# The opening of a hybrid attention block, from the norm to the rotary product, as named pieces in a written order

## The chip, the core and the metric

The kernel runs on one core of a Trainium2 chip. A core has five engines that run side by side: TensorE (PE) for matmuls, with its weight loads shown as PEld; VectorE (DVE), ScalarE (ACT) and GpSimd (POOL) for everything elementwise; SyncE (SP), which here issues transfers (DMA). Each engine works through its own list in order and waits for the others by semaphores. Matmul results land in PSUM; the other data lies in SBUF. The metric is the device time of one execution in microseconds; a profile shows one such execution.

## What is computed

One decoder layer with two attention branches over 528 tokens (16 meta tokens, then 512 real ones) of width 1024, in fp32:

```python
u = rmsnorm(h, pre_norm_g)
proj = u @ w_in
(cq, ckv, k_pe_raw, z_mla, fq, fk, fv, f_logit, z_fox, gate_a, gate_b) = jnp.split(proj, split_idx, axis=-1)
q = rmsnorm(cq, mla_q_norm_g) @ w_uq          # 16 heads, 64 plain + 32 rotary
kv = rmsnorm(ckv, mla_kv_norm_g) @ w_ukv
o_mla = causal_block_attention(q_m, k_m, v_mla, MLA_SCALE)
y_mla = (o_mla * silu(z_mla)) @ w_br_mla
cum = cumsum(log_sigmoid(f_logit + fox_forget_b))
o_fox = causal_block_attention(fq, fk, fv, FOX_SCALE, cum)
y_fox = (o_fox * silu(z_fox)) @ w_br_fox
mixed = (sigmoid(gate_a) * y_mla + sigmoid(gate_b) * y_fox) @ w_out
h = h + rmsnorm(mixed, post_norm_g)
```

## The kernel before

Products are made in split precision: an operand is cast to a rounded high half on ACT (`wh`, `uTh`, L142, L379), the difference is its low half (`wl`, `uTl`, made by `split_lo`, L118), and each product is three matmuls: high by high, low by high, high by low. All matmuls are recorded in the helper at L92, all PE transposes at L95, so the profile's tile names tell them apart.

The **opening** runs up to the first attention scores (`st`). It treats the tokens in five tiles: 0 to 3 with 128 real tokens each, 4 with the 16 meta tokens.

- `front(t)` (L351) sums the squares of a tile's rows on ACT (L361, L367), takes the root, multiplies the rows by its reciprocal and by the gain vector `gb` on DVE (`hn`, L370), turns them by eight PE transposes (`pt`) and splits the result into `uTh` and `uTl`.
- `gb` is the gain vector read from DRAM once for each of the 128 partitions, by two transfers ahead of the first weights (L320).
- `back(t)` (L382) multiplies a tile with the 432 columns of the small projection (q rank, kv rank, rotary key, forget gate) into `psm`: 24 matmuls, for each of eight k the three passes. These weights come in four loads of two k each (`wsr`, L326), with halves `wsh` and `wsl`. Then come the norms of the two ranks and the rotation of the key (`sm`, `tm`), and four transposes back (`pc`), from which `cTh`, `cTl`, `kpT` (rotary key) and `fT` (forget gate) are filled.
- Steps of head pair 0's query and key (`fq`, `fk`, eight k with three matmuls each; `fk` in two halves of the tokens) are run between the last tiles.
- The forget gate's cumulative sum (`fa`, L427 to L435) is stored to `CT`, which the fourth set of score matmuls reads.
- Behind that come the values of pair 0 (`v`, with a power-of-two scale from the largest value, L606 to L614), one output gate (`pg`, with its tanh) and the rotary part of eight heads' queries (`ppe`), whose four products with the rotary table are made on DVE (`gT`, L561).

Weights of 1024 columns come by `wload` (L120) into three slots (`wraw`) that the first three tiles of x also use; `wsplit` (L138) makes the halves, the low one on POOL unless told otherwise. Loads are asked for a few units ahead.

In the opening, a scheduler orders each engine's list, by the order in which the code is written and by the priorities given (`high_priority`). From the first attention stage on, PE's list is as written, and in the first stage the other engines' lists too.

Of the kernel before, what the change touches and what calls it, by code (L numbers as in the profile page):

```python
# [54 lines left out]
def block_kernel(ctx: ExitStack, tc: tile.TileContext, x, meta_tokens, pre_norm_g, w_in, fox_forget_b,  # L55
# [236 lines left out]
    lctx = ExitStack()  # L292
    with ExitStack() as ph:
        pa = ph.enter_context(tc.tile_pool(name="pa", bufs=2))
        pa1 = ph.enter_context(tc.tile_pool(name="pa1", bufs=1))
        pal = lctx.enter_context(tc.tile_pool(name="pal", bufs=1, side="right"))
        ppt = ph.enter_context(tc.tile_pool(name="ppt", bufs=2, space=PSUM))
        pps = ph.enter_context(tc.tile_pool(name="pps", bufs=2, space=PSUM, side="right"))
        warm = pa1.tile([1, 16], F32, tag="warm", name="warm")
        nc.scalar.activation(warm[:, 0:1], eps_t[0:1, 0:1], AF.Sqrt)  # L300

        hts = {}
        halves = (slice(0, 512), slice(512, D))

        def load_h(t):

            pool, tag = (wp, "wraw") if t < 3 else (pa, "ht")
            hts[t] = pool.tile([128, D], F32, tag=tag, name=f"ht{t}")
            if t == 0:
                for sl in halves:  # L310
                    nc.sync.dma_start(hts[t][:, sl], x2[0:128, sl])
            elif t < 4:
                nc.sync.dma_start(hts[t], x2[128 * t : 128 * t + 128])
            else:
                nc.sync.dma_start(hts[t][0:META], meta_tokens)

        load_h(0)
        gb = pa1.tile([128, D], F32, tag="gb", name="gb")
        for sl in halves:
            nc.sync.dma_start(gb[:, sl], pre_norm_g[0:1, sl].broadcast_to([128, 512]))  # L320
        wsh = pa1.tile([128, KD, NSM], F32R, tag="wsh", name="wsh")
        wsl = pa1.tile([128, KD, NSM], F32R, tag="wsl", name="wsl")
        nsm0 = NSM - NH
        for c in range(4):
            r = pa.tile([128, 2, NSM], F32, tag="wsr", name=f"wsr{c}", bufs=4)
            nc.sync.dma_start(r[:, :, 0:nsm0], win[:, 2 * c : 2 * c + 2, 0:nsm0])  # L326
            nc.sync.dma_start(r[:, :, nsm0:], win[:, 2 * c : 2 * c + 2, O_F : O_F + NH])
            if c == 1:
                load_h(1)
            hi = wsh[:, 2 * c : 2 * c + 2, :]  # L330
            nc.scalar.copy(hi, r)
            split_lo((nc.gpsimd, nc.vector)[c % 2], wsl[:, 2 * c : 2 * c + 2, :], r, hi)
        for t in (4, 2, 3):
            load_h(t)
        gq = pa1.tile([128, R_Q + R_KV], F32, tag="gq", name="gq")
        nc.sync.dma_start(gq[:, 0:R_Q], mla_q_norm_g[0:1].broadcast_to([128, R_Q]))
        nc.sync.dma_start(gq[:, R_Q:], mla_kv_norm_g[0:1].broadcast_to([128, R_KV]))
        rt = pa1.tile([128, 5, 4, 16], F32, tag="rt", name="rt")
        nc.sync.dma_start(rt, rope_tok)
        fb = pa1.tile([NH, 1], F32, tag="fb", name="fb")  # L340
        nc.sync.dma_start(fb, fox_forget_b.rearrange("a h -> h a"))
        fa = pal.tile([NH, 3, L], F32, tag="fa", name="fa")
        nc.gpsimd.memset(fa[:, 2], 0.0)
        fT = pal.tile([NH, L], F32, tag="fT", name="fT")
        kpT = pal.tile([ROPE, L], F32, tag="kpT", name="kpT")

        def rstd(dst, ss, n, epsc, rows):
            nc.scalar.activation(dst, ss, AF.Sqrt, bias=eps_t[:rows, epsc : epsc + 1], scale=1.0 / n)
            nc.vector.reciprocal(dst, dst)

        def front(t):  # L351
            rows, d0 = (128, META + 128 * t) if t < 4 else (META, 0)
            ht = hts[t]
            hn = pa.tile([128, D], F32, tag="hn", name=f"hn{t}")
            st1 = pa.tile([128, 16], F32, tag="st1", name=f"st1_{t}")
            parts = [slice(0, D)]
            if t == 0:

                parts = halves
                for i, sl in enumerate(parts):  # L360
                    nc.scalar.activation(hn[:, sl], ht[:, sl], AF.Square, accum_out=st1[:, 2 + i : 3 + i])  # L361
                nc.vector.tensor_scalar(out=st1[:, 0:1], in0=st1[:, 2:3], scalar1=1.0 / D, scalar2=EPS, op0=ALU.mult,
                                        op1=ALU.add)
                nc.scalar.activation(st1[:, 1:2], st1[:, 3:4], AF.Sqrt, bias=st1[:, 0:1], scale=1.0 / D)
                nc.vector.reciprocal(st1[:, 1:2], st1[:, 1:2])
            else:
                nc.scalar.activation(hn[:rows], ht[:rows], AF.Square, accum_out=st1[:rows, 0:1])  # L367
                rstd(st1[:rows, 1:2], st1[:rows, 0:1], D, 0, rows)
            for sl in parts:
                nc.vector.scalar_tensor_tensor(out=hn[:rows, sl], in0=ht[:rows, sl], scalar=st1[:rows, 1:2],  # L370
                                               in1=gb[:rows, sl], op0=ALU.mult, op1=ALU.mult)
            for half in range(2):
                pt = ppt.tile([128, 4, 128], F32, tag="pt", name=f"pt{t}_{half}")
                for kk in range(4):
                    k = 4 * half + kk
                    tps(pt[:, kk, :rows], hn[:rows, 128 * k : 128 * k + 128], ident[:rows, :rows])
                dh = uTh[:, 4 * half : 4 * half + 4, d0 : d0 + rows]
                dl = uTl[:, 4 * half : 4 * half + 4, d0 : d0 + rows]
                nc.scalar.copy(dh, pt[:, :, :rows])  # L379
                split_lo(nc.vector, dl, pt[:, :, :rows], dh)  # L380

        def back(t):  # L382

            rows, d0, q0 = (128, META + 128 * t, 0) if t < 4 else (META, 0, R_Q)
            psm = pps.tile([128, NSM], F32, tag="psm", name=f"psm{t}")
            passes(psm[:, q0:], lambda k: uTh[:, k, d0 : d0 + 128], lambda k: uTl[:, k, d0 : d0 + 128],
                   lambda k: wsh[:, k, :], lambda k: wsl[:, k, :], KD, slice(q0, NSM))
            sm = pa.tile([128, NSM], F32, tag="sm", name=f"sm{t}")
            st2 = pa.tile([128, 16], F32, tag="st2", name=f"st2_{t}")
            for a, b, i in ((0, R_Q, 0), (R_Q, R_Q + R_KV, 1)):  # L390
                if a < q0:
                    continue
                nc.scalar.activation(sm[:rows, a:b], psm[:rows, a:b], AF.Square, accum_out=st2[:rows, i : i + 1])
                rstd(st2[:rows, 2 + i : 3 + i], st2[:rows, i : i + 1], b - a, 0, rows)
                nc.vector.scalar_tensor_tensor(out=sm[:rows, a:b], in0=psm[:rows, a:b], scalar=st2[:rows, 2 + i : 3 + i],
                                               in1=gq[:rows, a:b], op0=ALU.mult, op1=ALU.mult)
            k0 = R_Q + R_KV
            tm = pa.tile([128, 2, 2, 16], F32, tag="tm", name=f"tm{t}")
            for i in range(2):
                for cs in range(2):  # L400
                    nc.vector.tensor_tensor(out=tm[:rows, i, cs], in0=psm[:rows, k0 + 16 * i : k0 + 16 * i + 16],
                                            in1=rt[:rows, t, 2 * i + cs], op=ALU.mult)
# [16 lines left out]
        for f, t in ((front, 0), (front, 1), (back, 0), (front, 4), (front, 2), (back, 1), (front, 3), (back, 2)):  # L419
            f(t)  # L420
        run(qk[:3])
        back(3)
        run(qk[3:7])
        back(4)


# [816 lines left out]
```

## Time and profile before

| | |
|---|---|
| runs shown | 623.45, 625.56, 625.99 us (median 625.56) |
| the profiled execution | 623.18 us, of it 621.3 us span |
| granted TensorE clock | 0.997 |
| first transpose on PE | 7.78 us |
| first scores (`st`) on PE | 72.45 us |
| bytes moved | 85.15 MB, 137 GB/s over the span |

In the profile's rows a time is in microseconds from the span's start. A timeline row gives start, duration, engine, line, operation, what it writes and reads, and in brackets how long the engine stood idle before it and what ended that. A row of stretches gives the length, the busy time of PE, PEld, DVE, ACT and POOL (each with its number of instructions), the granted clock, the share of time that the DMA engines were busy, and GB/s.

### The profile page before, as it was taken

To read this page: it belongs to the slowest core of one execution; us is meant where nothing else is said; L and a number is where in the kernel's file an instruction comes from. 1 tells how busy PE (TensorE), PEld (TensorE's weight loads), DVE (VectorE), ACT (ScalarE), POOL (GpSimd) and SP (SyncE) were. 2 spreads that over 40 slices of the span, in tenths; PEclk is the share of its full clock that TensorE was granted. 3 is DMA by queue.
4 is the path that set the end of the run, shared out by engine and by line. 5 is a ranking of instruction groups with operands and counts; after the bars stand their busy time and mean duration, and the time that the engine had idled before them with its cause. 6 is when DMAs were issued, how large, how long until landed. Compare 5 with 4: busy or idle time off the path is not lost.

```text
span 621.3 us, 11569 instructions
## 1 busy us (share of the span) xinstructions
PE 600.1 (97%) x4058; PEld 492.9 (79%) x4058; DVE 381.8 (61%) x1015; ACT 384.0 (62%) x838; POOL 188.9 (30%) x237
## 2 busy tenths in 40 slices
PE   3999999999999999999999999999999999999996
PEld 2879787978988889889889888887888865565885
DVE  3746668367466566674774774676977865556133
ACT  5656677379477576774884784776767654444421
POOL 3234544634444353352444353420000000003700
PEclk9999999999999999999999999999999999999998
DMA  8442576876666577467357586567252137332202
GB/s 284 129 85 52 128 139 175 188 192 163 161 136 140 142 148 157 125 167 180 97 142 172 137 145 161 137 162 216 66 157 80 35 89 250 101 111 93 102 34 103
DMA packets 204842, 85.15 MB, mean 137 GB/s; under 512 B 122788, under 2 KB 197924, under 8 KB 204784
## 3 DMA queue, kind: packets, MB, share of 16 engines
q1 hardware_dynamic: 204784, 84.41, 53.7%
q8 instruction: 32, 0.52, 0.4%
q14 instruction: 26, 0.21, 0.1%
HBM read 54.95 MB, written 4.00 MB: 95 GB/s over the span
## 4 chain that ended last, share of the span: by engine, by line
PE 88%; ACT 3%; DMA 3%; DVE 3%; POOL 2%; issue 1%; SPq 0%; DVEq 0%; ACTq 0%; POOLq 0%
PE pg L92 14%; PE z L92 13%; PE v L92 8%; PE st L92 7%; PE po L92 7%; PE fq L92 7%; PE fk L92 7%; PE py L92 6%; PE ov L92 5%; PE yx L92 3%; PE psm L92 3%; DMA wraw<-in_w_in_dram 2%; PE yy L92 2%; PE mq L92 2%; ACT wh L142 1%; PE mk L92 1%
## 5 line engine op out<-in xcount | busy, mean ns | idle before, releaser
L118 POOL TENSOR_TENSOR wl<-wraw,wh 128x1024 fp32r<-128x1024 f32 (+1 forms) x60 | 133.0, 2219 | 299.2 <-ACT wh L142 288.3
L142 ACT CAST wh<-wraw 128x1024 fp32r<-128x1024 f32 (+1 forms) x74 | 72.9, 986 | 84.8 <-issue 35.3
L708 ACT ACTIVATE sf<-sf,nb 128x144 f32<-128x144 f32 (+3 forms) x128 | 71.9, 565 | 3.4 <-DVE nb L698 3.4
L736 ACT ACTIVATE pn<-sf,ri 128x128 f16<-128x128 f32 (+3 forms) x128 | 61.9, 551 | 15.2 <-ACT sf L708 13.8
L737 DVE SCALAR_TENSOR_TENSOR pn<-sf,ri,pn 128x128 f16<-128x128 f32 (+3 forms) x128 | 65.6, 554 | 7.4 <-ACT pn L736 7.4
L92 PE MATMUL pg<-uTh,wh 128*128 128x512 f32 x128 | 51.9, 406 | 0.0
L92 PE MATMUL z<-uTh,wh 128*128 128x512 f32 x128 | 50.9, 398 | 0.0
L92 PE MATMUL z<-uTh,wl 128*128 128x512 f32 x128 | 50.1, 392 | 0.0
L92 PE MATMUL z<-uTl,wh 128*128 128x512 f32 x128 | 50.1, 391 | 0.0
L92 PE MATMUL pg<-uTh,wl 128*128 128x512 f32 x128 | 50.0, 391 | 0.0
L92 PE MATMUL pg<-uTl,wh 128*128 128x512 f32 x128 | 49.9, 390 | 0.0
L92 PE MATMUL st<-hlk,hlq 64*128 64x272 f32 (+3 forms) x480 | 48.6, 307 | 1.1 <-DVE nb L698 0.9
L698 DVE CUSTOM_DVE_ANT_0 sf<-st,maskt 128x272 f32<-128x272 f32 (+2 forms) x128 | 48.4, 434 | 0.0
L92 PE MATMUL py<-g,yw 128*128 128x512 f16 x192 | 42.6, 379 | 0.6 <-DVE yw L1006 0.6
L92 PEld LDWEIGHTS st<-hlk,hlq 64*128 64x128 f32 x480 | 35.7, 185 | 8.1 <-DVE nb L698 2.6
L92 PE MATMUL fk<-uTl,wh 128*128 128x256 f32 (+1 forms) x128 | 36.6, 286 | 0.0
L92 PE MATMUL v<-uTh,wh 128*128 128x256 f32 (+1 forms) x128 | 36.5, 285 | 0.0
L92 PE MATMUL fk<-uTh,wh 128*128 128x256 f32 (+1 forms) x128 | 36.5, 285 | 0.0
L92 PE MATMUL fk<-uTh,wl 128*128 128x256 f32 (+1 forms) x128 | 36.5, 285 | 0.0
L92 PE MATMUL v<-uTl,wh 128*128 128x256 f32 (+1 forms) x128 | 36.4, 285 | 0.0
L92 PE MATMUL v<-uTh,wl 128*128 128x256 f32 (+1 forms) x128 | 36.4, 285 | 0.0
L92 PEld LDWEIGHTS <-yw 128*128 128x128 f16 x192 | 17.8, 97 | 22.7 <-DVE yw L1006 1.1
(291 smaller groups left out, 1503.3 us busy)
## 6 DMA issues: line engine op xcount, KB each, us to landing
wraw<-in_w_in_dram SPq DMA_DIRECT2D x56, 512.0 KB
yraw<-in_w_br_fox_dram SPq DMA_DIRECT2D x8, 512.0 KB
yraw<-in_w_br_mla_dram SPq DMA_DIRECT2D x8, 512.0 KB
wraw<-in_w_out_dram SPq DMA_DIRECT2D x8, 512.0 KB
pt<-pn SPq DMA_TRANSPOSE x128
xr<-in_x_dram SPq DMA_DIRECT2D x4, 512.0 KB
out_dram<-yo SPq DMA_DIRECT2D x8, 256.0 KB
QP<-qpe_dram SPq DMA_DIRECT2D x7, 256.0 KB
```

The costliest lines, as they stand in the source:

```text
L92: nc.tensor.matmul(*a, **k)
L118: eng.tensor_tensor(out=lo, in0=src, in1=f32(hi), op=ALU.subtract)
L142: nc.scalar.copy(wh[:, :n], raw[:, :n])
L698: nc.vector.tensor_tensor_reduce(out=sf_of(h, b)[:, c0 : c0 + w], in0=ps[h][:, o : o + w], in1=maskt[:, m0 : m0 + w], scale=-scale, scalar ...
L708: nc.scalar.activation(sf, sf, AF.Exp, bias=sums["nb"][:, h, b : b + 1], scale=-1.0, accum_out=sums["su"][:, h, b : b + 1])
L736: nc.scalar.activation(hi, sf, AF.Copy, scale=rib)
L737: nc.vector.scalar_tensor_tensor(out=lo, in0=sf, scalar=rib, in1=hi, op0=ALU.mult, op1=ALU.subtract)
```

## The change

The scheduler no longer orders the opening. Every step is a small function with a name, and three lists of names (`OPENING`, `MIDDLE`, `LAST`; 205, 48 and 4 names) are run through in order, with all five engines' lists as issued. `front` and `back` become a class `Tile` with one method for each piece. The names: `Sq` sum of squares, `sr` root, `hn` scaled rows, `pt` transposes of half a tile (a, b), `uh`/`ul` the halves of u, `wh`/`wl` with a digit the halves of the small weights' four parts, `hh`/`lh`/`hl` two matmuls of the small projection (u's half, weight's half, tile, part), `qs qn ks kn tm kc` the norms, rotation and gate columns, `pc` the transposes back, `ch cl kf` what is filled from them; `L`, `wh`, `wl` with a letter q, k, v, g, p, z the load and halves of a large weight.

```diff
+    OPENING = (
+        "Sq0a Sq0 rc0 hn0a wh0 hn0b Lq pt0a wl0 uh0a pt0b wh1 ul0a hh00 uh0b wl1 lh01 Sq1 hl00 ul0b hl01 sr1 "
+        "wh2 hn1 Lk hh01 wh3 hh02 lh02 wl3 lh03 Sq4 wl2 hh03 pt1a sr4 pt1b hn4 uh1a hl03 Sq2 hh10 hl11 ul1a "
...
+        "lh30 kf2 fq5 cl2 qs3 tm3 fq6 ks3 qn3 fq7 kc3 kn3 fk10 hq fk11 pc3 whg lq fk12 fk13 kf3 wlg fk14 fk15 "
+        "ch3 fk16 ab fk17 cl3"
+    ).split()
+    MIDDLE = (
+        "Lz Lr ex v00 kph v01 mem v02 v03 v04 v05 hk1 v06 lnf v07 v10 lk1 v11 vr0 v12 v13 whp st v14 v15 wlp "
+        "v16 v17 scan pg0 whz pg1 vr1 chc pg2 wlz vs pg3 chl Lm Lb vT pg4 kpl pg5 vz pg6 pg7"
+    ).split()
...
+        ph.enter_context(tc.manual_schedule(engines={E_.PE, E_.Activation, E_.DVE, E_.Pool, E_.SP}))
...
+        grow = pa1.tile([1, D], F32, tag="grow", name="grow")
+        nc.scalar.dma_start(grow, pre_norm_g[0:1])
...
+        dark = acc("dark")
+        for _ in range(4):
+            mm(dark, ALL1, ALL1.unsqueeze(1).broadcast_to([128, 4, 128]), start=True, stop=True)
+        gb = [acc(f"gb{i}") for i in range(2)]
+        for i, sl in enumerate(halves):
+            mm(gb[i], one, grow[:, sl], start=True, stop=True)
...
+        for name in OPENING:
+            do[name]()
```

Four things change beside the order. The gain vector is loaded as one row (`grow`) on ACT's queue and spread over the partitions by two plain fp32 matmuls with a column of ones, into two PSUM buffers that hold it until tile 3 is scaled; the spread load is gone. Four bf16 matmuls of ones with ones (`dark`), whose result nothing reads, stand first on PE. The low halves of the weights of query, key, value, gate and rotary product, and of the third part of the small weights, are made on DVE instead of POOL. The z weight of the first attention stage is loaded and split ahead of that stage instead of in it.

The list of SP, which issues the loads, began so before:

```order
L311 DMA ht_125<-in_x_dram 128x512 x2
L320 DMA gb<-in_pre_norm_g_dram 128x512 x2
L326 DMA wsr_133<-in_w_in_dram 128x2x416
L327 DMA wsr_133<-in_w_in_dram 128x2x16
L326 DMA wsr_138<-in_w_in_dram 128x2x416
L327 DMA wsr_138<-in_w_in_dram 128x2x16
L313 DMA ht_141<-in_x_dram 128x1024
```

and begins now, still on SP at the program's start:

```order
L450 DMA ht_131<-in_x_dram 128x512 x2
L461 DMA wsr_134<-in_w_in_dram 128x2x416
L462 DMA wsr_134<-in_w_in_dram 128x2x16
L461 DMA wsr_137<-in_w_in_dram 128x2x416
L462 DMA wsr_137<-in_w_in_dram 128x2x16
L452 DMA ht_140<-in_x_dram 128x1024
```

The two transfers of `gb` are gone; the weights' first part follows x directly.

PE's list began with tile 0's transposes and took each k's three passes in turn:

```order
L95 MATMUL pt_0_181<-ident,hn_172 128x128 x4
L95 MATMUL pt_1_188<-ident,hn_172 128x128 x4
L92 MATMUL psm_215<-wsh,uTh 128x432
L92 MATMUL psm_215<-wsl,uTh 128x432
L92 MATMUL psm_215<-wsh,uTl 128x432
L92 MATMUL psm_215<-wsh,uTh 128x432
```

and now, at the same place:

```order
L92 MATMUL gb_173<-grow,one 128x512
L92 MATMUL gb_174<-grow,one 128x512
L95 MATMUL pt_0_189<-ident,hn_177 128x128 x4
L95 MATMUL pt_1_196<-ident,hn_177 128x128 x4
L92 MATMUL psm_203<-wsh,uTh 128x432 x2
L92 MATMUL psm_203<-wsh,uTl 128x432 x2
L92 MATMUL psm_203<-wsl,uTh 128x432 x4
L92 MATMUL psm_203<-wsh,uTh 128x432 x4
L92 MATMUL psm_203<-wsh,uTl 128x432 x4
L92 MATMUL psm_203<-wsh,uTh 128x432 x2
L95 MATMUL pt_0_241<-ident,hn_210 128x128 x4
L95 MATMUL pt_1_247<-ident,hn_210 128x128 x4
```

The order within a tile now follows the halves: 18 of tile 0's products stand ahead of tile 1's transposes, where 13 stood before, and the low weights come when their part is split.

On ACT, which makes the high halves, the rows behind tile 0's sum of squares were:

```order
L331 CAST wsh<-wsr_133 128x864
L331 CAST wsh<-wsr_138 128x864
L379 CAST uTh<-pt_0_181 128x4x128
L379 CAST uTh<-pt_1_188 128x4x128
L367 ACTIVATE hn_195,st_1_196<-ht_141 128x1024
```

and are now:

```order
L489 CAST wsh<-wsr_134 128x864
L554 CAST uTh<-pt_0_189 128x4x128
L489 CAST wsh<-wsr_137 128x864
L554 CAST uTh<-pt_1_196 128x4x128
L529 ACTIVATE hn_210,st_1_211<-ht_140 128x1024
```

The first half of tile 0 is cast as soon as the first part of the weights is, ahead of the second part.

More of the change, by code (lines that the diff above doesn't have):

```diff
@@ L288, in k_fox @@
         return unit(f"fk{pr}", win_w(O_FK, pr), u_act, KD, ALLT, done)
[L292 to L402, printed above, removed]
-            nc.vector.tensor_tensor(out=sm[:rows, k0 : k0 + 32].rearrange("p (a b) -> p a b", a=2), in0=tm[:rows, 0],
-                                    in1=tm[:rows, 1], op=ALU.add)
-            nc.scalar.copy(sm[:rows, k0 + 32 :], psm[:rows, k0 + 32 :])
-            pc = pps.tile([128, 4, 128], F32, tag="pc", name=f"pc{t}", bufs=1)
-            i0 = q0 // 128
-            for i in range(i0, 3):
-                tps(pc[:, i, :rows], sm[:rows, 128 * i : 128 * i + 128], ident[:rows, :rows])
-            tps(pc[0 : ROPE + NH, 3, :rows], sm[:rows, k0:NSM], ident[:rows, :rows])
-            ds = slice(d0, d0 + rows)
-            nc.scalar.copy(cTh[:, i0:3, ds], pc[:, i0:3, :rows])
-            split_lo(nc.vector, cTl[:, i0:3, ds], pc[:, i0:3, :rows], cTh[:, i0:3, ds])
-            nc.scalar.copy(kpT[:, ds], pc[0:ROPE, 3, :rows])
-            nc.scalar.activation(fT[:, ds], pc[ROPE : ROPE + NH, 3, :rows], AF.Identity, bias=fb)
-        qk = q_fox(0) + k_fox(0)
[L419 to L424, printed above, removed]
-        nc.scalar.activation(fa[:, 0], fT, AF.Abs)
-        nc.scalar.activation(fa[:, 0], fa[:, 0], AF.Exp, scale=-1.0)
-        nc.scalar.activation(fa[:, 0], fa[:, 0], AF.Ln, bias=1.0)
-        nc.vector.scalar_tensor_tensor(out=fa[:, 1], in0=fT, scalar=0.0, in1=fa[:, 0], op0=ALU.min, op1=ALU.subtract)
-        nc.vector.tensor_tensor_scan(out=fa[:, 0], data0=fa[:, 1], data1=fa[:, 2], initial=0.0, op0=ALU.add,
-                                     op1=ALU.add)
-        ch = pal.tile([NH, 2, L], F32R, tag="ch", name="ch")
-        nc.scalar.activation(ch[:, 0], fa[:, 0], AF.Copy, scale=-1.0 / SC_FOX)
-        nc.vector.scalar_tensor_tensor(out=ch[:, 1], in0=fa[:, 0], scalar=-1.0 / SC_FOX, in1=f32(ch[:, 0]),
-                                       op0=ALU.mult, op1=ALU.subtract)
-        for i in range(2):
-            for h in range(2):
-                nc.sync.dma_start(f32(CT[64 * h + i : 64 * h + i + 1, :]), f32(ch[h : h + 1, i]))
-        for i in range(2):
-            nc.sync.dma_start(c_dram[i], f32(ch[:, i]))
-        run(qk[7:])
@@ L473, in __init__, with put, fn, rope_w @@
             self.steps[0][1].load = w.load
-    E_ = mybir.EngineType
+    later = {}
+    def put(names):
+        def fn(i, *fns):
+            later.update(zip(names[i], fns))
+        return fn
+    q0, k0 = q_fox(0, put([("hq", "lq")])), k_fox(0, put([("hk0", "lk0"), ("hk1", "lk1")]))
+    g0 = gate_unit()
+    wv0 = win_w(O_FV, 0)
+    wuqh = wuq.rearrange("p k (h e) -> p k h e", e=NOPE + ROPE)
+    def rope_w(g):
+        return weights(lambda: [wuqh[:, k, 8 * g : 8 * g + 8, NOPE + 16 * x : NOPE + 16 * x + 16]
+                                for x in range(2) for k in range(2)], lambda ws: ws)
@@ new lines, in block_kernel, with hi, fn, lo @@
+    wp0 = rope_w(0)
+    lows, made = {}, {}
+    def hi(name, make, eng):
+        def fn():
+            lows[name] = []
+            made[name] = make(eng, lows[name])
+        return fn
+    def lo(name):
+        def fn():
+            for f in lows[name]:
+                f()
+        return fn
+    for name, get, make, eng in (("q", q0[0][1], q0[0][1].make, nc.vector), ("k", k0[0][1], k0[0][1].make, nc.vector),
+                                 ("v", wv0, wv0, nc.vector), ("g", g0[0][1], g0[0][1].make, nc.vector),
+                                 ("p", wp0, wp0, nc.vector)):
+        later.update({"L" + name: get.load, "wh" + name: hi(name, make, eng), "wl" + name: lo(name)})
@@ new lines, in block_kernel, with ab, ex, lnf @@
+    for k in range(KD):
+        later[f"fq{k}"] = q0[k][1]
+        later[f"pg{k}"] = g0[k][1]
+        for i in range(2):
+            later[f"fk{i}{k}"] = k0[KD * i + k][1]
+    def ab():
+        nc.scalar.activation(fa[:, 0], fT, AF.Abs)
+    def ex():
+        nc.scalar.activation(fa[:, 0], fa[:, 0], AF.Exp, scale=-1.0)
+    def lnf():
+        nc.scalar.activation(fa[:, 0], fa[:, 0], AF.Ln, bias=1.0)
+    def st_():
+        nc.vector.scalar_tensor_tensor(out=fa[:, 1], in0=fT, scalar=0.0, in1=fa[:, 0], op0=ALU.min, op1=ALU.subtract)
@@ L556, in pe_unit @@
             for xi in range(2):
[L557 removed]
+                get = (lambda: half(1)) if xi else get0 and (lambda: half(0, get0())) or weights(srcs, lambda ws: half(0, ws))
                 def done(i, ps, xi=xi):
@@ L812, in block_kernel @@
         mgates = [Gate() for _ in gates[:]]
-        ahead(first + sum(fills, []) + tail + mgates[0].steps)
-        run(first)
+        za, q, zb = early
+        later.update(whz=hi("z", za.make, nc.gpsimd), wlz=lo("z"), Lz=za.load, Lm=q.load, Lb=zb.load, mem=mem, kph=kph,
+                     kpl=kpl, Lr=lambda: nc.sync.dma_start(rope0_t, rope_pe))
+        for k in range(KD):
+            for i in range(2):
+                later[f"v{i}{k}"] = v0[KD * i + k][1]
+        with tc.manual_schedule(engines={E_.PE, E_.SP, E_.Pool, E_.Activation, E_.DVE}):
+            for name in MIDDLE:
+                later[name]()
+            lctx.close()
+            gT = [gctx[b].enter_context(tc.tile_pool(name=f"gp{b}", bufs=1, side="right")).tile(
+                [128, KD, S], F32, tag=f"gT{b}", name=f"gT{b}") for b in range(2)]
+            pe, *rope0 = pe_unit(0, lambda: made["p"])
+            for x in range(2):
+                for k in range(2):
+                    later[f"pp{x}{k}"] = pe[2 * x + k][1]
+            for name in LAST:
+                later[name]()
+        pe, pe_turn, pe_rest, _ = pe_unit(1)
+        fills[1][9:9] = pe + [(0, pe_turn)] + [(0, lambda x=x: pe_rest(x)) for x in (1, 0)]
+        ahead(sum(fills, []) + tail + mgates[0].steps)
         late = []
```

323 lines of the change are left out of this document (270 added, 53 removed), and 6 rows, old and new, of the table OPENING.

## The prediction, made before the changed kernel had run

> **What bounds the kernel now.** I read the page first: its busy line and the chain that ended last.
>
> ```profile
> span 621.3 us, 11569 instructions
> PE 600.1 (97%) x4058; PEld 492.9 (79%) x4058; DVE 381.8 (61%) x1015; ACT 384.0 (62%) x838; POOL 188.9 (30%) x237
> ...
> PE 88%; ACT 3%; DMA 3%; DVE 3%; POOL 2%; issue 1%; SPq 0%; DVEq 0%; ACTq 0%; POOLq 0%
> ```
>
> The reader sees a kernel that TensorE (PE) carries throughout: 621.3 - 600.1 = 21.2 us of its span hold no matmul. Next come the busy times by stretch. The opening ends at 72.45, where the first scores (st) start.
>
> ```profile
> 0.00:20.00 20.00, 9.20 (x30) 7.59 (x31) 9.18 (x11) 9.55 (x17) 7.43 (x16) 1.00 0.88 289
> 20.00:72.45 52.45, 50.71 (x306) 44.09 (x304) 32.13 (x82) 32.77 (x84) 17.54 (x17) 1.00 0.33 81
> ```
>
> The first figure behind the length is PE's: half of the 21 us without a matmul (20 - 9.20 = 10.8) lies in the first 20 us, and only 1.74 in the 52 us behind it. So the change, which ends at the first scores, can win much only at the very start. PE's timeline there shows a second loss:
>
> ```profile
> 7.78 2.04 PE L95 MATMUL pt<-ident,hn 128*128 128x128 f32 x8 [7.78 <-DVE hn L370]
> 12.05 0.73 PE L92 MATMUL psm<-wsh,uTh 128*128 128x432 f32 x1 [2.23 <-ACT uTh L379]
> ...
> 13.98 0.73 PE L92 MATMUL psm<-wsh,uTl 128*128 128x432 f32 x1 [0.79 <-DVE uTl L118]
> 14.50 0.56 PE L92 MATMUL psm<-wsh,uTh 128*128 128x432 f32 x1
> 14.86 0.56 PE L92 MATMUL psm<-wsl,uTh 128*128 128x432 f32 x1
> ...
> 18.10 1.91 PE L95 MATMUL pt<-ident,hn 128*128 128x128 f32 x8
> ...
> 20.08 0.36 PE L92 MATMUL psm<-wsh,uTl 128*128 128x432 f32 x1
> 20.27 0.36 PE L92 MATMUL psm<-wsh,uTh 128*128 128x432 f32 x1
> ```
>
> Equal products start 0.36 us apart at 14.5 and 0.19 at 20: up to about 20 PE runs at half speed, though the granted clock reads 1.00. It speeds up after 6.1 us without a pause (13.98 to 20.08). By 20.08 fourteen products and 16 transposes had started, and the twentieth ends near 21.25 (six more by 0.195). I use that point, **tile 0's 20th product with two tiles transposed**, as the mark of comparison. Behind it come these pauses:
>
> ```profile
> 29.71 0.66 PE L95 MATMUL pt<-ident,hn 128*128 128x128 f32 x4 [0.25 <-DVE uTl L118]
> ...
> 30.84 0.66 PE L95 MATMUL pt<-ident,hn 128*128 128x128 f32 x4 [0.28 <-DVE uTl L118]
> ...
> 33.30 0.41 PE L95 MATMUL pc<-ident,sm 128*128 128x128 f32 x2 [0.24 <-DVE sm L395]
> ...
> 37.40 0.27 PE L95 MATMUL pc<-ident,sm 128*48 128x128 f32 x1 [0.80 <-DVE sm L403]
> ...
> 46.52 0.41 PE L95 MATMUL pc<-ident,sm 128*128 128x128 f32 x2 [0.15 <-DVE sm L395]
> ```
>
> Together 1.72 us: 0.53 for a transpose buffer (pt), 1.19 for a token tile's normed row (sm). From the mark to st, 72.45 - 21.25 = 51.2 us, PE therefore works 49.5.
>
> **The change, part by part.** *The gain vector (gb) comes by two matmuls instead of a spread load.* Rows of VectorE (DVE), two stretches whose last number is GB/s, rows of ScalarE (ACT), POOL and DVE:
>
> ```profile
> 5.07 0.16 DVE L365 RECIPROCAL st<-st 128x1 f32<-128x1 f32 x1 [0.79 <-ACT st L364]
> 6.88 0.75 DVE L370 SCALAR_TENSOR_TENSOR hn<-ht,st,gb 128x512 f32<-128x512 f32 x1 [1.65 <-DMA gb<-in_pre_norm_g_dram]
> ```
> ```profile
> 2.00:3.00 1.00, 0.00 (x0) 0.00 (x0) 0.00 (x0) 0.20 (x1) 0.08 (x1) 1.00 0.99 371
> 4.00:5.00 1.00, 0.00 (x0) 0.00 (x0) 0.15 (x1) 0.97 (x5) 0.00 (x0) 1.00 0.51 111
> ```
> ```profile
> 3.38 0.63 ACT L361 ACTIVATE hn<-ht 128x512 f32<-128x512 f32 x1 [1.17 <-DMA ht<-in_x_dram]
> ...
> 9.38 0.91 ACT L331 CAST wsh<-wsr 128x864 fp32r<-128x864 f32 x1 [4.35 <-DMA wsr<-in_w_in_dram]
> ...
> 11.42 1.06 ACT L379 CAST uTh<-pt 128x512 fp32r<-128x512 f32 x2
> 12.37 1.07 ACT L367 ACTIVATE hn<-ht 128x1024 f32<-128x1024 f32 x1
> ```
> ```profile
> 10.38 2.03 POOL L118 TENSOR_TENSOR wsl<-wsr,wsh 128x864 fp32r<-128x864 f32 x1 [8.30 <-ACT wsh L331]
> ```
> ```profile
> 13.24 1.27 DVE L118 TENSOR_TENSOR uTl<-pt,uTh 128x512 fp32r<-128x512 f32 x2
> ...
> 14.62 1.29 DVE L370 SCALAR_TENSOR_TENSOR hn<-ht,st,gb 128x1024 f32<-128x1024 f32 x1
> ```
>
> DVE has its scale at 5.23 and waits for gb until 6.88. Meanwhile DMA falls from 371 to 111 GB/s. Without those 0.52 MB the first weights (wsr, 0.44 MB at 370) follow x directly: x lands by 4.0, weights at about 5.2 instead of 9.38, the next every 1.2 us, each tile of x 1.4. The one-row load (grow) is smaller than half of x, which lands at 3.38; I take that as its end. No row shows a plain fp32 product: between 0.43 us (432 columns in 0.36, for 512) and 1.02 (a transpose of 128 columns in 2.04/8). I take 1.02, as it too is fp32: both are done at 5.4, ahead of the 5.98 at which PE is wanted, so they cost nothing. The four warming products (dark) lie ahead of them.
>
> [...]
>
> *The walk to the mark*, each piece at its row's price. hn 5.23 to 5.98 and 6.7; transposes (0.255 each) to 7.0 and 8.0. ACT: wh0 to 6.1, uTh 7.0 to 7.5, wh1 8.4, uTh 8.9, square of tile 1 and root 10.2, wh2 11.1, wh3 12.0, then tile 4's square to 13.3. POOL's wsl: 6.1 to 8.2. DVE: wl1 8.4 to 9.5, hn of tile 1 10.2 to 11.6, wl3 12.0 to 13.1. PE: first product at **7.5** (12.05 before), the second pair at 8.4, and from there no pause: pairs of 0.72 end at 9.1, 9.9, 10.6, 11.3, 12.0, 12.7, 13.5, 14.2. If the speed again comes after 6.1 us without a pause, it comes at 14.5; tile 1's transposes end near 15.2 and the 20th product at **15.6**. That is 21.25 - 15.6 = **5.65 us** won.
>
> [...]
>
> *The low halves of five weights, and one more of the small ones, go from POOL to DVE.*
>
> ```profile
> 81.92 1.21 DVE L118 TENSOR_TENSOR wl<-wraw,wh 128x1024 fp32r<-128x1024 f32 x1
> ```
> ```profile
> 24.27 0.67 PE L95 MATMUL pt<-ident,hn 16*128 16x16 f32 x8
> ...
> 51.65 0.29 PE L92 MATMUL fk<-uTh,wh 128*128 128x272 f32 x1
> 51.77 0.29 PE L92 MATMUL fk<-uTl,wh 128*128 128x272 f32 x1
> ```
>
> Four such, one of half the width and one of 864 columns are 6.4 us more on DVE. DVE is busy 32.13 of the 52.45 us, so they fit; what they can do is delay a piece behind them. From 12.0 on, DVE's row up to tile 3's hn is wl3, wl2, hn4, two uTl, hn2, wlq, wlk, hn3 and 0.3 of small ones: 1.0 + 1.0 + 1.4 + 1.3 + 1.4 + 1.2 + 1.2 + 1.4 + 0.3 = 10.2, with some 0.7 of waits 22.9. PE comes to that transpose at 15.6 + fourteen pairs at 0.39 + tile 4's transposes 0.67 + tile 2's 1.0 (half of 1.91) + six fk pieces of three at 0.12 = 24.9. Cover: 2 us; beyond it each us costs one.
>
> *The pauses behind the mark.* The two waits on pt (0.53) go: between a tile's halves the list puts other products. For the waits on sm I see no row of the new order, so bounds: 0, as the list has 2.8 to 3.1 us of products ahead of the pc of tiles 2 and 3, and twice today's 1.19. I take 1.19 again, the value of the rows of that kind: **0.53 us** won.
>
> *The forget-gate chain* (fa, L427 to L435, then CT), with the scale of v that now stands ahead of its end:
>
> ```profile
> 54.89 0.65 ACT L427 ACTIVATE fa<-fT 16x528 f32<-16x528 f32 x1
> ...
> 64.09 0.40 PE L92 MATMUL pg<-uTh,wh 128*128 128x512 f32 x1
> ...
> 64.93 0.70 DVE L435 SCALAR_TENSOR_TENSOR ch<-fa,ch 16x528 fp32r<-16x528 f32 x1 [0.71 <-ACT ch L434]
> ...
> 66.97 0.16 DVE L614 RECIPROCAL vsc<-vsc 128x1 f32<-128x1 f32 x1
> ...
> 72.45 0.56 PE L92 MATMUL st<-hlk,hlq 64*128 64x144 f32 x6
> ```
> ```profile
> L440 SPq DMA_DIRECT2D CT<-ch x4: 534/583/638, 64.9 to 66.9; - x4
> ```
>
> 10.7 us from start to end; st follows 6.8 later. In the list its last step stands behind the peak of v's second half, and v ends 8.4 us ahead of st (64.09 to 72.45 are gate and rotary product). Peak and scale at most 1.5 (65.63 to 67.13), this step 0.7, two of CT's issues 1.2, a landing under 3.4 (x's, from the program's start): 6.8. Cover: at least 1.6 us. Table loads, kpT copies (KPH) and the z weight's halves, now ahead of st, lie beside v and pg. Behind st all engines keep their order but for one cast and one load, so the rest moves as a whole.
>
> **Sum:** 5.65 + 0.53 = 6.2 us. The profiled execution took 623.18, so 617.0. That execution is 2.4 under the median of the runs shown, 625.56 (623.45 to 625.99); by the median it would be 619.4. I predict the middle, **618.0**.
>
> **Rivals.** (a) *The half speed lasts*: if pauses reset it and it ends only at 18, the mark comes at 17.0; 4.3 + 0.5 = 4.8 won, 618.4 (620.8 by the median). For it: the 2.23 us pause before 12.05. Against: from 8.4 on nothing pauses. (b) *In-order rows give part back*: each ACT and DVE piece now waits at the head of its row. Fourteen handovers behind the mark (six half tiles, five pc, three psm buffers) at 0.2 us (the small pauses above are 0.15 to 0.28) cost 2.8: 3.4 won, 619.8. (c) *Hidden anyway*: PE arrives early but st waits for CT; should the chain overrun its cover by 4.5 us, 1.7 are won, 621.5. Against: the cover, and a landing that is far smaller than x's. (d) *Slower*: v's weight (Lv) loads only when tile 2's hn has freed its slot, at 18.8, and its cast stands in ACT's row ahead of tiles 0 and 1's norms and tile 3's uTh. In before loads queued on slots long:
>
> ```profile
> SPq L133 <- POOL wl L118: 31.3, 6, 17.3
> ```
>
> Landing after 24.9 costs PE us for us; past 31.1 the whole gain is gone. A 17.3 us hold there means landing near 39, 14.1 late: 7.9 lost net, 631.1. Against: the slot is freed by DVE, whose row has cover, and DMA moves 81 GB/s there.
>
> **How the numbers follow.** A measurement tells about 0.5% (3.1 us) from no change. Forecast 0.57, (a) 0.15, (b) 0.14, (c) 0.10, (d) 0.04. Faster: forecast, (a) and three quarters of (b): 0.82; same: the rest of (b), (c) and a little more: 0.14; slower 0.04. The range runs from the best case (full speed from the first product, mark near 13.7, no sm waits: 9.3 won, 613.9) to (b) by the median, 622.2: 614.0 to 622.2.
>
> **What would show it.** First psm near 7.5; spacing 0.36 until 11 to 15; the mark near 15.6; st near 66.3; PE's idle between them near 1.2. Wrong, if psm starts after 9.5, if PE idles over 3 us between mark and st, or if the stretch from st to the end is not the 548.9 us of before.

## The result, and the profile after

The changed kernel took 618.99 us (median of four runs, 618.08 to 619.91), the kernel before 625.16 beside it (four runs): a ratio of 0.9905, 95% interval 0.9879 to 0.9931. Measured twice more on other occasions it came to 0.9939 (0.9919 to 0.9959) and 0.9938 (0.9916 to 0.9960). By these ratios the change is worth 5.9 us on the first occasion and 3.8 to 3.9 on the two others. Predicted were 618.0, between 614.0 and 622.2, so the time is as forecast. The way to it is not: the opening won more than was forecast, and a good part was lost again behind it.

| | before | predicted | after |
|---|---|---|---|
| profiled execution, of it span | 623.18, 621.3 | 617.0 (by the profile of before) | 619.91, 618.0 |
| first product (`psm`) | 12.05 | 7.5 | 8.51 |
| mark (tile 0's 20th product, two tiles transposed) | 21.25 | 15.6 | 15.15 |
| first scores (`st`) | 72.45 | 66.3 | 63.77 |
| from `st` to the end of the span | 548.9 | 548.9 | 554.3 |

The page of the changed kernel's profile, its first lines and the clock by fortieths of the span:

```profile
span 618.0 us, 11583 instructions
...
PEclk9999979999999999999999999999999999999998
```

The clock has a dip, a 7 in the sixth slice, at 77 to 93 us; before, its first 39 slices read 9. Stretches of the changed kernel say where (length, busy time of PE, PEld, DVE, ACT, POOL, clock, DMA share, GB/s):

```profile
15.15:63.77 48.62, 48.32 (x299) 43.61 (x298) 35.53 (x89) 31.02 (x80) 6.30 (x11) 1.00 0.30 71
...
76.20:79.27 3.07, 0.00 (x1) 0.00 (x0) 3.07 (x7) 3.07 (x9) 0.15 (x1) 0.84 0.24 58
79.27:85.13 5.86, 5.86 (x17) 4.93 (x18) 3.85 (x9) 4.06 (x9) 2.88 (x5) 0.50 0.78 172
```

From the mark at 15.15 to the first scores PE stands still for only 0.30 us (48.62 - 48.32). Then, 12.4 us into the first attention stage, it stands still for 3.07 us, and for the 5.86 us behind that it has half the clock. PE's timeline of the changed kernel, first in the opening, then around the pause:

```profile
3.01 3.78 PE L92 MATMUL gb<-grow,one 1*128 1x512 f32 x4
6.72 2.02 PE L95 MATMUL pt<-ident,hn 128*128 128x128 f32 x8
8.51 1.09 PE L92 MATMUL psm<-wsh,uTh 128*128 128x432 f32 x2
9.39 0.91 PE L92 MATMUL psm<-wsh,uTl 128*128 128x432 f32 x2
10.13 1.10 PE L92 MATMUL psm<-wsl,uTh 128*128 128x432 f32 x4
11.07 0.56 PE L92 MATMUL psm<-wsh,uTh 128*128 128x432 f32 x2
11.99 0.66 PE L92 MATMUL psm<-wsh,uTh 128*128 128x432 f32 x2 [0.36 <-ACT wsh L489]
...
14.51 0.64 PE L92 MATMUL psm<-wsl,uTh 128*128 128x432 f32 x2
15.46 0.66 PE L92 MATMUL psm<-wsh,uTh 128*128 128x432 f32 x2 [0.30 <-ACT uTh L554]
...
79.27 0.80 PE L92 MATMUL z<-uTh,wl 128*128 128x512 f32 x1 [3.07 <-DVE wl L118]
...
91.46 0.39 PE L92 MATMUL st<-hlk,hlq 64*128 64x272 f32 x1 [0.42 <-DVE nb L898]
```

Two products take 0.88 us at 8.51 and four take 0.94 at 10.13, so full speed comes at about 10 already. The two of 14.51 end at 15.15; they are the 19th and 20th.

The same work in the kernel before, from the product that had not to wait to the second of the next scores:

```profile
84.71 0.39 PE L92 MATMUL z<-uTh,wl 128*128 128x512 f32 x1
...
94.12 0.39 PE L92 MATMUL st<-hlk,hlq 64*128 64x272 f32 x1 [0.41 <-DVE nb L698]
```

(`z<-uTh,wl` is a product with the low half of the z weight, `wl`.) It took 94.12 - 84.71 = 9.41 us there and 91.46 - 79.27 = 12.19 in the changed kernel: the half clock costs 2.8, on top of the pause's 3.07.

Why does DVE's `wl` come late? Following the releasers back through the changed kernel, on DVE, ACT and SP (SP's row of waits gives the time in all, how often, the longest):

```profile
74.41 0.17 DVE L917 TENSOR_SCALAR su<-su 128x6 f32<-128x6 f32 x1 [5.46 <-ACT sf L908]
...
78.00 1.21 DVE L118 TENSOR_TENSOR wl<-wraw,wh 128x1024 fp32r<-128x1024 f32 x1
```
```profile
66.82 0.62 ACT L142 CAST wh<-wraw 128x512 fp32r<-128x512 f32 x1 [5.14 <-DMA wraw<-in_w_ukv_dram]
69.23 1.05 ACT L142 CAST wh<-wraw 128x1024 fp32r<-128x1024 f32 x1 [1.79 <-DMA wraw<-in_w_in_dram]
70.19 0.41 ACT L908 ACTIVATE sf<-sf,nb 128x144 f32<-128x144 f32 x1
```
```profile
57.11 1.26 SPq L394 DMA_DIRECT2D CT<-ch  x2
...
61.87 2.14 SPq L133 DMA_DIRECT2D wraw<-in_w_uq_dram  x2
64.06 0.98 SPq L133 DMA_DIRECT2D wraw<-in_w_ukv_dram  x2
65.09 1.09 SPq L133 DMA_DIRECT2D wraw<-in_w_in_dram  x2
```
```profile
SPq L394 <- ACT ch L392: 8.1, 1, 8.1
```

DVE waits for ACT's `sf`; that row starts at 70.19, behind two casts that wait for loads; the loads (`Lm`, `Lb` in the list) were issued at 61.87 to 66.2, because on SP they stand behind the stores of `CT`, and SP stood 8.1 us at the first of these until ACT had made `ch`. Before, the same loads were issued ahead of the stores, from 55.25 on:

```profile
56.69 0.95 SPq L133 DMA_DIRECT2D wraw<-in_w_ukv_dram  x2
62.19 0.37 SPq L133 DMA_DIRECT2D wraw<-in_w_in_dram  x1
64.92 2.53 SPq L440 DMA_DIRECT2D CT<-ch  x4
```

That is the theory that the first experiments were to test: **the loads behind CT's stores** cost the pause, and the pause costs the clock.

### The profile page after: what moved, and what is told of

It reads as the page before. It is cut to its first block, busy times and chain, and to the rows that moved or that the text cites. A ratio compares the mean times of both kernels' runs of the same rounds, so it can differ in the third digit from the quotient of the medians.

```text
span 618.0 us, 11583 instructions
## 1 busy us (share of the span) xinstructions
PE 604.8 (98%) x4066; PEld 494.7 (80%) x4066; DVE 384.1 (62%) x1025; ACT 384.2 (62%) x838; POOL 176.6 (29%) x232
## 4 chain that ended last, share of the span: by engine, by line
PE 86%; DVE 4%; ACT 3%; DMA 2%; issue 2%; POOL 1%; SPq 1%; DVEq 0%; ACTq 0%; POOLq 0%
PE pg L92 13%; PE z L92 12%; PE st L92 7%; PE po L92 7%; PE fq L92 7%; PE v L92 7%; PE fk L92 6%; PE py L92 6%; PE ov L92 5%; PE yx L92 3%; PE psm L92 3%; PE yy L92 2%; PE mq L92 1%; PE mk L92 1%; DMA qpe_dram<-gT 1%
## 5 line engine op out<-in xcount | busy, mean ns | idle before, releaser
L118 POOL TENSOR_TENSOR wl<-wraw,wh 128x1024 fp32r<-128x1024 f32 (+1 forms) x55 | 122.2, 2225 | 276.0 <-ACT wh L142 264.0
```

Source lines behind the costliest of these rows:

```text
L118: eng.tensor_tensor(out=lo, in0=src, in1=f32(hi), op=ALU.subtract)
```

## The experiments

The changed kernel once more, and a version in which nothing moves but the two loads:

```diff
-        "Lz Lr ex v00 kph v01 mem v02 ... whp st v14 v15 wlp "
-        "v16 v17 scan pg0 whz pg1 vr1 chc pg2 wlz vs pg3 chl Lm Lb vT pg4 ..."
+        "Lz Lr Lm ex v00 kph v01 mem v02 ... whp st v14 v15 wlp Lb "
+        "v16 v17 scan pg0 whz pg1 vr1 chc pg2 wlz vs pg3 chl vT pg4 ..."
```

> The changed kernel again, nothing edited. Theory: the loss behind the first scores is built into the order. PE stands about 3.1 us near 76 ahead of a product z<-uTh,wl that waits for DVE's wl, and the stretch of half granted clock of about 6 us that follows (78 to 85 in the first profile) is set off by that pause. So the pause comes again within 0.3 us, a stretch at half clock comes again behind it, st starts within 1 us of 63.8 and the time lies between 617.5 and 620. Rival: the clock's fall was an accident of that one execution and has nothing to do with the pause; then the pause is there without it, or a fall stands at another place, and the span is nearer 615.5 than 618.

> The loads of the weights for mq/mk (Lm) and of the second z weight (Lb) are asked for ahead of CT's stores on SP instead of behind them; nothing else moves. Theory: in the changed kernel SP stands 8.1 us ahead of CT's first store, these loads behind it, ACT's two casts behind the loads, and sf behind the casts (70.19, though its first input is there at 65.4); so the low half on DVE is late and PE stands 3.07 us and then runs at half clock for some 6 us. With the loads at about 49.5 and 55.5, sf starts near 65.4, wl ends near 74.5, ahead of the 76.0 at which PE wants it; no pause, no half clock, span near 612.6, time 613.5 to 615.5, a ratio to before near 0.983. Rival: the casts and sf are late for another reason (ACT's or DVE's own rows); then the loads land early, sf still starts after 69, the pause stays over 2 us and the time stays at 618 to 620.

The unedited kernel had its pause again, 2.53 us ending at 78.69 (shorter than expected), `st` at 63.74; its time, 621.47, was above what was expected. Its stretches around the pause, and a second one at half clock further on:

```profile
76.16:78.69 2.53, 0.00 (x0) 0.00 (x1) 2.53 (x5) 2.53 (x8) 0.00 (x0) 1.00 0.18 45
78.69:79.78 1.09, 1.09 (x5) 0.91 (x6) 1.05 (x4) 1.05 (x5) 0.65 (x4) 1.00 0.40 90
79.78:83.19 3.41, 3.41 (x12) 2.84 (x11) 2.71 (x5) 2.65 (x5) 0.86 (x2) 0.50 0.67 165
...
134.39:137.80 3.41, 3.41 (x12) 2.96 (x11) 1.30 (x4) 0.71 (x1) 0.00 (x0) 0.50 0.92 208
```

The half clock comes with the pause again, here 1.1 us after PE has resumed, and lasts 3.41 us. (In the first profile it began within the pause: a mean of 0.84 over 3.07 us is 1.0 us at half clock, with the 5.86 behind it 6.8.) The second stretch, at 134.39, stands behind two short pauses of 0.63 and 0.86 us at the products `mk`; the first profile has one of 0.67 there and no such stretch. So a long pause is not needed for it. With the loads moved, SP and then ACT and DVE read:

```profile
49.95 0.88 SPq L133 DMA_DIRECT2D wraw<-in_w_uq_dram  x2
...
55.74 0.37 SPq L133 DMA_DIRECT2D wraw<-in_w_in_dram  x1
57.66 1.25 SPq L394 DMA_DIRECT2D CT<-ch  x2
```
```profile
65.97 0.42 ACT L908 ACTIVATE sf<-sf,nb 128x144 f32<-128x144 f32 x1 [0.69 <-DVE nb L898]
```
```profile
73.79 1.21 DVE L118 TENSOR_TENSOR wl<-wraw,wh 128x1024 fp32r<-128x1024 f32 x1
```

All as the theory had it: loads at 49.95 and 55.74, `sf` at 65.97 waiting for nothing but its input, the low half done at 75.0, no pause and no half clock behind it. The same holds over all profiles: in the seven with the loads behind the stores (this kernel three times, and four versions of it) PE stands 2.5 to 4.2 us at this product, in the four with the loads moved it doesn't stop there.

The time is 617.61, ratio 0.9898 (0.9876 to 0.9919): 3.9 us under the changed kernel beside it, but above the 613.5 to 615.5 that were expected. In the profile the stretch from `st` to the end takes 550.4, against 554.3 in the first profile of the changed kernel and 548.9 before, and `st` comes 0.55 later. Where the rest stays the version's timeline shows, on PE, ACT and SP:

```profile
128.52 0.40 PE L92 MATMUL mk<-cTh,wh 128*128 128x272 f32 x1 [1.20 <-DVE sil L851]
...
130.02 0.39 PE L92 MATMUL mk<-cTh,wh 128*128 128x256 f32 x1 [0.85 <-DVE hlq L118]
```
```profile
114.73 1.05 ACT L142 CAST wh<-wraw 128x1024 fp32r<-128x1024 f32 x1 [6.58 <-DMA wraw<-in_w_in_dram]
```
```profile
99.32 11.41 SPq L944 DMA_TRANSPOSE pt<-pn  x8
110.83 1.16 SPq L133 DMA_DIRECT2D wraw<-in_w_in_dram  x2
```

Two pauses of 2.05 together, where before had one of 0.86 and the changed kernel's first profile one of 0.67: a cast again waits for a load, and this load stands on SP behind eight transposes that wait for the attention weights. PE comes there 4.9 us earlier than in the first profile of the changed kernel (127.32 and 132.19), the load only 3.3 (110.83 and 114.17). This link is read from the trace; moving that load was not tried.

Next the parts of the change, one undone at a time: the gain by its spread load again, and the low halves on POOL again (v, g and p as q and k).

```diff
...
+        gbt = pa1.tile([128, D], F32, tag="gb", name="gb")
+        for sl in halves:
+            nc.sync.dma_start(gbt[:, sl], pre_norm_g[0:1, sl].broadcast_to([128, 512]))
...
-        for i, sl in enumerate(halves):
-            mm(gb[i], one, grow[:, sl], start=True, stop=True)
```
```diff
-    ("q", q0[0][1], q0[0][1].make, nc.vector), ("k", k0[0][1], k0[0][1].make, nc.vector),
+    ("q", q0[0][1], q0[0][1].make, nc.gpsimd), ("k", k0[0][1], k0[0][1].make, nc.gpsimd),
...
-            do[f"wl{c}"] = lambda c=c: w_lo(c)
+            do[f"wl{c}"] = lambda c=c: w_lo(c, (nc.vector, nc.gpsimd)[c == 2])
```

> The gain vector comes by the spread load of before again (two transfers of 0.26 MB behind x's first tile, ahead of the weights); the row load and the two matmuls are gone, the four warming products stay, the order is that of the changed kernel. Theory: the spread load delays the first weights from 6.5 to about 9.4; first product near 11.5 instead of 8.51, the mark (tile 0's 20th product with two tiles transposed) near 18 to 19 instead of 15.1, st 2.5 to 4 us later than 63.8, time 620.5 to 623. Rival: the written order alone brings the gain and the weights' landing hardly matters; then st stays within 1 us of 63.8 and the time within 1 us of the changed kernel's.

> The low halves of the five large weights of the opening and of the third part of the small weights are made on POOL again, at the same places of the list. Theory: POOL's 2.4 us against DVE's 1.2 make the halves late at their places in the list, and the loads that wait for their slots with them; PE pauses between the mark and st by 2 us or more in all, st at 66 or later, time 621 or more. Rival: POOL is idle enough, and DVE, freed of 6.4 us, makes up for it: st within 1 us of 63.8, time within 1 us of the changed kernel's.

With the spread load the first product starts at 11.58, the mark is at 19.21, `st` at 67.44, 3.7 later; the time is 623.01, ratio 0.9987 (0.9973 to 1.0001). The theory holds, with the mark a little past its 18 to 19 and the time at the edge of its 620.5 to 623. Its ACT row for the first weights, and the pause behind `st` with the stretch that follows it:

```profile
10.13 0.91 ACT L489 CAST wsh<-wsr 128x864 fp32r<-128x864 f32 x1 [4.64 <-DMA wsr<-in_w_in_dram]
```
```profile
82.60 0.50 PE L92 MATMUL z<-uTh,wl 128*128 128x512 f32 x1 [2.73 <-DVE wl L118]
```
```profile
82.60:95.18 12.58, 11.59 (x85) 9.08 (x85) 9.81 (x34) 10.30 (x27) 7.11 (x8) 1.00 0.95 163
```

The landing at 10.1 instead of 6.5 is what it costs. This version also speaks against a simple link from pause to clock: the pause of 2.73 is there, and the clock stays at 1.00 for 12.6 us behind it; a stretch of 3.41 us at half clock comes only at 95.18, where PE has stood for no more than 0.2 to 0.4 us at a time. With the low halves on POOL, `st` is at 65.72, 1.9 later (2.2 or more were expected), the time 622.04 (0.9967, 0.9949 to 0.9985). Half of the theory holds: pauses between mark and `st` are only 0.59 (2 or more were expected); 0.9 is lost ahead of the mark, and the pause behind `st` grows to 4.15.

Then the reverse, one part alone: the kernel before with the gain's row and products and nothing else, and the changed kernel without the gain's products, the low halves on DVE and the warming products, so with the written order and the early z weight alone (its edit is the two above and the one that takes the warming products out).

```diff
...
-        gb = pa1.tile([128, D], F32, tag="gb", name="gb")
-        for sl in halves:
-            nc.sync.dma_start(gb[:, sl], pre_norm_g[0:1, sl].broadcast_to([128, 512]))
+        gb = [acc(f"gb{i}") for i in range(2)]
+        for i, sl in enumerate(halves):
+            mm(gb[i], one, grow[:, sl], start=True, stop=True)
...
```

> The kernel before with one part of the change alone: the gain vector as one row spread by two fp32 products into two PSUM buffers; its scheduler still orders the opening, POOL still makes the low halves. Theory (the landing of the weights is the larger part of the 6.3 us at the mark): weights' cast at 6.5 to 7 instead of 9.38, first product near 8.5 to 9, st 2.5 to 4.5 earlier than 72.45, time 1.5 to 4.5 us under before, ratio 0.993 to 0.998. Rival: the scheduler's order gives it all back (PSUM buffers held for the gain are taken from the query's and key's products), st within 1 us of 72.45, ratio 0.999 to 1.002.

> The changed kernel with three parts undone at once: the gain vector by the spread load, the low halves on POOL, no warming products. What is left is the written order with the z weight's load ahead of the first stage. Theory: parts add up; the gain's load costs 3.7 at st and the low halves 1.9 against 63.8, so st near 69.4, 3 us ahead of before's 72.45, and with the loss behind st the time lies within 2 us of before, 623 to 626. Rival: the order needs the parts (a piece that is late holds the whole row), st after 71, time above 626.

Neither part is worth anything alone. The gain's products in the kernel before give 623.43, ratio 0.9994 (0.9975 to 1.0012); `st` comes 1.3 earlier, the first product at 13.82, later than before. The weights do land early (cast at 6.78). But the scheduler's row on DVE, in that version:

```profile
9.18 1.58 DVE L118 TENSOR_TENSOR wsl<-wsr,wsh 128x864 fp32r<-128x864 f32 x1 [3.17 <-ACT wsh L335]
10.81 0.16 DVE L353 RECIPROCAL st<-st 128x1 f32<-128x1 f32 x1
10.93 1.41 DVE L374 SCALAR_TENSOR_TENSOR hn<-ht,st,gb 128x512 f32<-128x512 f32 x2
```

Tile 0's rows, whose inputs were there at 6.1, are scaled at 10.93, behind a weight's low half and tile 1's root: with the gain early, the scheduler orders DVE so that it waits elsewhere. Whether the two PSUM buffers held for the gain cost anything, as the rival had it, is not shown. The order alone is slower than before: 629.78, ratio 1.0092 (1.0069 to 1.0116), `st` at 73.45 and not 69.4. The two costs from above (3.7 and 1.9) do not simply add: together the parts give 9.7. On PE and ACT of that version:

```profile
33.83 0.90 PE L95 MATMUL pc<-ident,sm 128*128 128x128 f32 x4 [2.30 <-DVE sm L601]
```
```profile
31.95 1.04 ACT L142 CAST wh<-wraw 128x1024 fp32r<-128x1024 f32 x1 [3.57 <-DMA wraw<-in_w_in_dram]
```

v's cast, at the head of ACT's row, waits for a late load and holds the norm behind it: rival (d) of the prediction, in this version. PE then has half its clock for 3.41 us (0.50 from 35.55 to 38.96), an estimated 1.7 us more.

What brings full speed at the start was tried by leaving out the four warming products, and by letting the gain's products run over all 128 rows (127 of them zero) in the version with the loads moved:

```diff
-        dark = acc("dark")
-        for _ in range(4):
-            mm(dark, ALL1, ALL1.unsqueeze(1).broadcast_to([128, 4, 128]), start=True, stop=True)
```
```diff
-        grow = pa1.tile([1, D], F32, tag="grow", name="grow")
-        nc.scalar.dma_start(grow, pre_norm_g[0:1])
+        grow = pa1.tile([128, D], F32, tag="grow", name="grow")
+        nc.vector.memset(grow, 0.0)
+        nc.scalar.dma_start(grow[0:1], pre_norm_g[0:1])
...
-        one = pa1.tile([1, 128], F32, tag="one", name="one")
+        one = pa1.tile([128, 128], F32, tag="one", name="one")
...
-        for _ in range(4):
+        for _ in range(6):
```

> The changed kernel without the four warming products (dark); all else stays. In the five traces so far the clock became full at 10.0 to 13.0 where the gain's one-row products ran from 3.0 to 6.8, and never within those. Theory: the one-row products do not count towards the clock, so what stands ahead of them cannot either; the warming products buy nothing. Without them the gain's products still start near 3.0, first product 8.4 to 8.7, full speed (product spacing 0.19 to 0.24 instead of 0.43) between 9.5 and 13.5, st between 63.2 and 65. Rival: the warming products bring the clock up early; without them full speed comes after 13.5 and st after 65.2.

> The version with the loads ahead of CT's stores, and in it the gain's row stands in a tile of 128 rows of which the other 127 are zero, so that the two products that spread it run over all 128 rows of the array; the tile is cleared on DVE first, so its load is asked for about 1 us later, and six warming products instead of four bridge to it. Theory: full-array products count towards the clock, one-row products do not; with PE busy from 1.2 on, full speed comes between 4.6 and 8.4 instead of 10 to 13, the transposes and first products run at full speed, the mark falls from 15.1-15.7 to 13.5-14.5, st to 62.5-63.3, time 0.5 to 2 us under the version with the loads alone. Rival: what kept the clock half open was the fp32 products as such, or a fixed time from the program's start; then full speed comes after 9.4 again, the mark is later than 15 by what the later load costs, and the time is the same or up to 1 us more.

Without the warming products the first product starts at 8.20, 0.3 earlier, and `st` is at 63.95 (one run, 619.73): in that profile they are not missed, and the pause behind `st` (3.20) is there as in the changed kernel. With 128 rows, PE's timeline of that version, and behind it the transposes and products of the version with the loads alone:

```profile
5.34 3.34 PE L92 MATMUL gb<-grow,one 128*128 128x512 f32 x4 [1.41 <-DMA grow<-in_pre_norm_g_dram]
8.52 0.60 PE L95 MATMUL pt<-ident,hn 128*128 128x128 f32 x4
```
```profile
7.62 1.11 PE L95 MATMUL pt<-ident,hn 128*128 128x128 f32 x4
...
10.20 1.94 PE L92 MATMUL psm<-wsl,uTh 128*128 128x432 f32 x4
11.93 1.36 PE L92 MATMUL psm<-wsh,uTh 128*128 128x432 f32 x4
```

Four transposes take 0.60 at 8.52 instead of 1.11 at 7.62: in this one profile full speed has come within 3.2 us of the start of the gain's products. With one row, 3.78 us of the same products did not bring it (the eight transposes behind them took 2.02 in the changed kernel's first profile, 2.04 before), and full speed came 3.3 to 6 us after the transposes began. The theory holds for the speed, not for the time: the row, asked for at 1.95 instead of 0.71, held the products up until 5.34 (loads were asked for ahead of it; that they delayed it is not shown), the mark came at 16.44, and the time is that of the version with the loads alone, 618.62 (0.9906, 0.9887 to 0.9925).

At last the changed kernel beside the version with the loads moved, with and without the warming products, on one chip:

> The changed kernel a third time, beside the two versions with the loads moved, on one chip: the two measurements so far, 0.9905 and 0.9939 of before, lie apart by as much as the step that is to be told. Theory: pause of 2.5 to 3.2 us ahead of z<-uTh,wl and a stretch at half clock behind it again; ratio 0.990 to 0.995. Rival: no pause, ratio under 0.988.

> The version with the loads ahead of CT's stores again, beside the changed kernel on one chip. Theory: 2.5 to 5 us under the changed kernel, ratio 0.985 to 0.991 to before, no pause ahead of z<-uTh,wl, clock 0.998 to 1.0 in its profile. Rival: what is won at that pause is lost at the next one (mk, near 129); the two kernels lie within 1.5 us.

> The loads ahead of CT's stores, and the warming products gone. Theory: the warming products only hold the gain's products up by the 0.3 us that were seen (first product 8.20 against 8.51), and the phase at which the clock opens is worth more than that; so the time is that of the version with the loads alone within 1 us, ratio 0.986 to 0.991, st between 63.4 and 64.8, no pause over 0.5 us between st and 85. Rival: without them the clock opens later than 13.5 and st is after 65, ratio above 0.991.

The changed kernel took 620.42 (0.9938, 0.9916 to 0.9960; pause 3.53, longer than expected), the loads ahead 618.68 (0.9895, 0.9875 to 0.9914), and without warming products 618.35 (0.9901, 0.9883 to 0.9918). So the version with the loads ahead beats both kernels, by 1.7 and 3.9 us against the changed one in the two comparisons of medians, by 2.6 and 2.7 if the ratios to before are taken. The theory asked for at least 2.5, its rival for at most 1.5: the 1.7 of this comparison lies between them, and the clock in the profile was 0.996, not 0.998 or more. (The changed kernel's first measurement, 0.9905 on another occasion, lies nearer to the version with the loads ahead.) The profile of that version from this comparison shows the rival's part, around the pauses at `mk`:

```profile
127.05:130.53 3.48, 1.14 (x7) 0.92 (x8) 2.58 (x6) 2.51 (x7) 2.36 (x1) 1.00 0.68 153
130.53:133.94 3.41, 3.41 (x13) 2.85 (x12) 0.67 (x3) 0.37 (x1) 0.00 (x0) 0.50 0.77 174
```

There, too, the clock is halved behind pauses: two of 1.72 and 0.86. The version without warming products has the same, 3.41 us at half clock behind 1.29 and 0.86.

## Why the prediction was right in the sum and not in its parts

1. *The gain by matmul.* The mechanism holds (3.7 us at `st`, by undoing it); two sizes were off. The weights were cast at 6.53, not 5.2, and the gain's two products took 3.78 us, not at most 2.04, and ended at 6.79 instead of 5.4. The bound from the nearest rows was too low. First product 8.51 instead of 7.5: 1.0 late.
2. *The walk to the mark.* "Speed after 6.1 us without a pause, at 14.5" was wrong: it came at about 10 here, at 11 to 13 in other executions of the same opening, and took back more than the late start had cost. Mark at 15.15, so 6.1 us won where 5.65 were forecast; a small pause on ACT (0.36) instead of none. (Read by the same ends, 20.86 + 0.55, the mark of before is 21.41 and not 21.25.) The 6.1 us were read from one profile, that of the kernel before; with 128 rows, full speed was there 3.2 us after a pause of 1.41 had ended. What sets the moment is not shown.
3. *The low halves on DVE.* Right: tile 3's rows are scaled by 23.32 (22.9 was said), PE transposes them at 25.28 without waiting (24.9), 2.0 us of cover. Undone, it costs 1.9 at `st`.
4. *The pauses behind the mark.* Mis-sized: all of them went, not 0.53 of them; one of 0.30 is new. I gave the waits on `sm` their old value; the list puts enough products ahead of each. From mark to `st` 48.6 us instead of 51.2, 2.6 won, and this is most of the difference at `st`. The pauses are 1.4 of it; the other 1.1 is that PE is busy for 48.3 us where it was for 49.5, in as many instructions (299). The prediction had no term for that, and why it is so is not shown.
5. *The forget gate's chain.* Right for what it was about: the last store to `CT` was issued by 60.74, and `st` did not wait for it.
6. *"The rest moves as a whole."* **The step that failed.** The order behind `st` is the same, but three loads that it consumes are issued ahead of `st`, and on SP they now stand behind `CT`'s stores. The prediction asked what the chain delays and looked at `st` alone; SP is a queue as well (it stood 8.1 us at `CT`'s first store), and what stands behind the waiting store was not named. It cost 3.07 and 2.8 us; from `st` to the end 5.4 more than before. By the prediction's own last sign (548.9 us from `st` to the end) this part was wrong.

So 8.7 us were won at `st` instead of 6.2, and 5.4 given back: 3.3 in the span, 6.2 predicted. That the median, 618.99, and the forecast, 618.0, lie so near is in part luck: a win larger than forecast and a loss that was left out pull against each other. In part it comes from the basis: the profile of before (623.18) was quicker than all four runs beside the result, that of the changed kernel (619.91) was the slowest of its four. On the two later occasions the changed kernel took 621.47 and 620.42.

Rivals: (a) and (b) fell, as full speed came early and PE stood for only 0.30 us between the mark and 63.77. (c) fell. (d) had the right mechanism, a cast in ACT's row that waits for a late load, at the wrong load: v's cast (23.32) waited for nothing, the two at 66.82 and 69.23 did.

## What to carry to other kernels

When an opening gets shorter, look at the first loads that the next stage consumes: here they started when SP came to them (the first at 61.87, and at 49.95 with the loads moved), and a store that waited 8.1 us for a result held the loads behind it in the same list. Put such loads ahead of stores that wait (here the time was then 3.9 and 1.7 us under that of the changed kernel), as soon as their slot is free. Parts of such a change (where an operand comes from, which engine makes it, the order) can be worth nothing alone (here 1.3 us won and 1.0 lost at the first scores) and 8.7 together; one part that brought nothing when tried is no proof against the whole.
